# Two hybrid decoder layers on one core: the scheduler orders all engines but TensorE by a timeline simulation

## The chip, the cores and the metric

The kernel runs on one core of one Trainium2 chip. The metric is device microseconds of one execution; the runs give 2353.19, 2354.23 and 2355.81 us, median 2354.23. A core has a matrix engine (TensorE, PE in the profile; PEld is its weight load), three engines for elementwise work (VectorE or DVE, ScalarE or ACT, GpSimd or POOL) and SyncE (SP), which here issues all DMAs. Each engine takes its instructions in the order in which they stand in its own program, and waits on semaphores for the others.

## The reference, cut to what matters

```python
# x (1, 1024, 1024) f32, two layers; 4 mLSTM heads and 4 retention heads of 256; chunks
for l in range(DEPTH):
    ada = c_act @ w_ada[l] + b_ada[l]
    shift, scale, gate = jnp.split(ada, 3, axis=-1)
    h = rmsnorm(x, norm_g[l]) * (1.0 + scale[:, None, :]) + shift[:, None, :]
    p = h @ w_in[l]
    mq, mk, mv, mo, mz, mi, mf, rq, rk, rv, rz = split_cols(p)
    qk = jax.nn.silu(causal_dwconv(jnp.concatenate([mq, mk], axis=-1), conv_w[l], conv_b[l]))
    cell = mlstm_chunkwise(...)            # scores, running state C, n, stabiliser m, per chunk
    y_m = jax.nn.sigmoid(mo) * head_layernorm(cell, gn_m[l], N_HEADS_MLSTM) * jax.nn.silu(mz)
    ret = retention_chunkwise(rotary(rq), rotary(rk), rv)   # scores with decay, running state R
    y_r = head_layernorm(ret, gn_r[l], N_HEADS_RET) * jax.nn.silu(rz)
    y = jnp.concatenate([y_m, y_r], axis=-1) @ w_out[l]
    x = x + gate[:, None, :] * y
return rmsnorm(x, final_g)
```

## The kernel before, in words

All products are made in about full f32 precision out of three matmuls (`mm3`, L134 to L136): each operand is split into a high part, which ScalarE casts to fp32r (L590), and the rest, which GpSimd (or in places VectorE) gets by a subtraction (L591). `split_to` does both, so nearly all splits have these two lines: weights (`raw` to `wH`, `wL`), scores (`sH`, `sL`), the running state (`cH`, `cL`), q and k (`b`).

A layer first normalises and transposes its input (`norm_scale` L291, `norm_transpose` L296, `norm_evac` L302/L304) into `hT`. Then come eight head groups `hg`, 0 to 3 mLSTM, 4 to 7 retention. Each has the products for the gates (`gate_path`, with `z_evac` L518/L520 and `o_evac` L529/L530, stored to `gdr` at L523 and L531), for q and k (`qk_ml` or `qk_ret`) and for v. The weights are loaded by `load_w_raw` on SP (L317) into four `raw` buffers and split into six `wH` and six `wL` buffers.

k goes through DRAM to be transposed: `k_store` writes `kdr` (L622), `k_rows` loads it back with four DMAs per chunk (L632) and splits it on ScalarE and VectorE (L641/L642 for mLSTM, L646/L648 for retention). `attention` takes four chunks of 256 rows: `scores(j)` (L742 in part, masked at L744 to L747), `values(j)` (evacuated at L788/L797/L799, statistics from L808, the variance at L818 to L825, normalised on ScalarE at L830), `update(j)` for the state (L766/L769), `finish(j)` to DRAM (`ndr`, L842). At the end of a layer `OutLoads` fetches the normalised rows and gates (L879, L880), multiplies and splits them (L882 to L886), and `out_units` makes the output product, which `out_evac` adds to x (L927 to L931). The last rows go out by `final_rows` (L960, L961, L966).

Generators carry this work: the products of one head group run as units (`run_units`), and after each unit `tick()` lets launched generators (attention of the previous group, k rows, the rotary tables during `hg` 1 of layer 0, the next layer's adaLN columns from `hg` 2 of layer 0 on, the output gate's rows from `hg` 5 on) write some of their own steps. So the text of the program interleaves the groups.

That written order is what TensorE executes: one line asks for it, and a second one does so for every engine during the startup:

```python
manual = ctx.enter_context(tc.manual_schedule(engines={mybir.EngineType.PE}))
startup = tc.manual_schedule()
startup.__enter__()
```

The startup holds the loads of x and of the first adaLN weights, and a `script` of some hundred short steps up to the first v weights of layer 0 (`startup.__exit__` follows it). After it, VectorE, ScalarE, GpSimd and SP are ordered by the framework's scheduler. It replays the program on a simulated machine; when an engine of that machine is free, it gets, of the instructions whose inputs and buffers are ready there, the one that stands earliest in the text. The order found so is written into each engine's program and does not change on the chip. The buffers of a pool (62 of the tag `b`, four `raw`, and so on) are given out along this replay, and so are the waits for buffers in use. One more constraint holds the four loads of the rotary tables (`load_rotary`) behind a store of head group 3 on SP. The simulated machine is the framework's default one, which carries its own estimate of each instruction's duration.

## Time and profile before

| what | value |
|---|---|
| runs | 2353.19, 2354.23, 2355.81 us |
| span of the profiled execution | 2353.8 us (the page gives no other time for it) |
| TensorE | 2307.7 us busy, 12597 matmuls |
| VectorE | 1289.8 us busy, 2699 instructions |
| ScalarE | 893.3 us busy, 1736 instructions |
| GpSimd | 882.8 us busy, 841 instructions |
| DMA | 260.50 MB, 111 GB/s on average |
| mean granted clock of TensorE | 0.994 |

A row of the waits names the waiting engine, tile and line, then who released it: the total in us, how often, the longest. A row of the timeline has its start and length in us, the engine, line and operation, the tile written and those read, and in brackets how long the engine stood idle before it and for whom. In a row of windows stand the stretch, its length, and the busy time of each engine with its number of instructions, then the granted TensorE clock, the share of the DMA engines in use, and GB/s. Numbers of buffers are left out of the names, so `b` stands for any of 62.

### The profile page before, as it was taken

What the parts mean: (1) busy time and instruction counts of PE and PEld (TensorE: products, weight loads), DVE (VectorE), ACT (ScalarE), POOL (GpSimd) and SP (SyncE); (2) the same over time, 40 slices, a digit from 0 to 9 for tenths busy, and PEclk for the clock granted to TensorE, in tenths of its full rate; (3) what the DMA queues carried; (4) which work ended last, traced back from release to release, by engine and by line L of the source; (5) the groups of instructions that cost most, each with busy time, mean ns of one, the idle gap of its engine ahead of it and who ended that gap; (6) DMA issues with size and microseconds to landing.
All of it is one profiled execution on the core that took longest, in us unless ns stands there. A gap on an engine that the chain in (4) does not pass through costs nothing.

```text
span 2353.8 us, 34446 instructions
## 1 busy us (share of the span) xinstructions
PE 2307.7 (98%) x12597; PEld 1982.2 (84%) x12597; DVE 1289.8 (55%) x2699; ACT 893.3 (38%) x1736; POOL 882.8 (38%) x841
## 2 busy tenths in 40 slices
PE   5999999999999999999999999999999999999998
PEld 4888888988978988988888888888898888888886
DVE  7375687656454445475525655454543444555753
ACT  5535443444332322343434444344443322224442
POOL 0344333443244343323453444343334434341313
PEclk8999999999999999999999999999999999999999
DMA  7223232434332433277422333322323242425762
GB/s 243 74 68 99 73 88 72 116 94 126 108 99 71 117 83 102 81 241 254 167 78 77 82 76 78 80 68 76 81 70 86 77 112 77 117 82 159 266 231 77
DMA packets 326971, 260.50 MB, mean 111 GB/s; under 512 B 75893, under 2 KB 262013, under 8 KB 326801
## 3 DMA queue, kind: packets, MB, share of 16 engines
q1 hardware_dynamic: 326800, 258.30, 37.4%
q8 instruction: 99, 1.62, 0.3%
q14 instruction: 72, 0.58, 0.1%
HBM read 202.61 MB, written 55.61 MB: 110 GB/s over the span
## 4 chain that ended last, share of the span: by engine, by line
PE 93%; DVE 2%; DMA 2%; issue 1%; POOL 1%; ACT 1%; SPq 1%; POOLq 0%; ACTq 0%; DVEq 0%
PE pp L134 24%; PE pp L136 24%; PE pp L135 24%; PE pa L136 6%; PE pa L134 6%; PE pa L135 6%; PE pa L742 1%; DMA b<-in_w_ada_dram 1%; DMA b<-in_x_dram 1%; PE pa L296 0%; DVE b L233 0%; DMA dm<-mdr 0%; POOL wL L591 0%; SPq L995 0%; POOL b L591 0%
## 5 line engine op out<-in xcount | busy, mean ns | idle before, releaser
L134 PE MATMUL pp<-b,wH 128*128 128x512 f32 x1792 | 712.7, 398 | 1.1 <-ACT b L1073 1.1
L135 PE MATMUL pp<-b,wH 128*128 128x512 f32 x1792 | 708.2, 395 | 1.3 <-DVE b L1076 1.3
L136 PE MATMUL pp<-b,wL 128*128 128x512 f32 x1792 | 708.2, 395 | 0.0
L591 POOL TENSOR_TENSOR wL<-raw,wH 128x512 fp32r<-128x512 f32 x338 | 449.2, 1336 | 578.5 <-ACT wH L590 506.5
L136 PEld LDWEIGHTS pp<-b,wL 128*128 128x128 f32 x1792 | 337.8, 189 | 81.0
L134 PEld LDWEIGHTS pp<-b,wH 128*128 128x128 f32 x1792 | 338.7, 189 | 74.1 <-issue 1.5
L135 PEld LDWEIGHTS pp<-b,wH 128*128 128x128 f32 x1792 | 338.4, 189 | 73.7 <-DVE b L1076 2.0
L590 ACT CAST wH<-raw 128x512 fp32r<-128x512 f32 x402 | 247.3, 617 | 390.4 <-PE pp L135 138.3
L136 PE MATMUL pp<-wH,b 128*128 128x256 f32 (+1 forms) x1152 | 353.0, 306 | 1.2 <-DVE b L886 1.1
L134 PE MATMUL pp<-wH,b 128*128 128x256 f32 (+1 forms) x1152 | 353.6, 307 | 0.0
L135 PE MATMUL pp<-wL,b 128*128 128x256 f32 (+1 forms) x1152 | 352.6, 306 | 0.0
L591 POOL TENSOR_TENSOR b<-acc,b 128x256 fp32r<-128x256 f32 (+1 forms) x208 | 200.4, 983 | 319.9 <-ACT b L590 306.0
L136 PEld LDWEIGHTS pp<-wH,b 128*128 128x128 f32 x1152 | 217.2, 189 | 13.5 <-DVE b L886 2.0
L134 PEld LDWEIGHTS pp<-wH,b 128*128 128x128 f32 x1152 | 216.9, 188 | 10.7
L135 PEld LDWEIGHTS pp<-wL,b 128*128 128x128 f32 x1152 | 216.6, 188 | 10.6
L590 ACT CAST b<-acc 128x256 fp32r<-128x256 f32 (+1 forms) x208 | 93.6, 487 | 201.5 <-DVE acc L685 136.5
L608 DVE SCALAR_TENSOR_TENSOR acc<-pp,cols,acc 128x511 f32<-128x511 f32 (+2 forms) x192 | 142.7, 743 | 44.2 <-ACT acc L603 42.0
L591 POOL TENSOR_TENSOR sL<-th,sH 128x384 fp32r<-128x384 f32 x64 | 69.5, 1086 | 155.4 <-ACT sH L590 141.2
L134 PE MATMUL pa<-wH,b 128*128 128x512 f32 x256 | 101.1, 395 | 0.0
L135 PE MATMUL pa<-wL,b 128*128 128x512 f32 x256 | 100.9, 394 | 0.0
L136 PE MATMUL pa<-wH,b 128*128 128x512 f32 x256 | 100.7, 393 | 0.0
L612 ACT ACTIVATE th<-acc 128x512 f32<-128x512 f32 x64 | 40.4, 632 | 146.6 <-DVE acc L610 79.8
(237 smaller groups left out, 3470.9 us busy)
## 6 DMA issues: line engine op xcount, KB each, us to landing
raw<-in_w_in_dram SPq DMA_DIRECT2D x274, 256.0 KB
raw<-in_w_out_dram SPq DMA_DIRECT2D x128, 256.0 KB
b<-in_w_ada_dram SPq DMA_DIRECT2D x96, 256.0 KB
gdr<-g SPq DMA_DIRECT2D x64, 256.0 KB
ndr<-zt SPq DMA_DIRECT2D x128, 128.0 KB
g<-ndr SPq DMA_DIRECT2D x64, 256.0 KB
g<-gdr SPq DMA_DIRECT2D x64, 256.0 KB
acc<-kdr SPq DMA_DIRECT2D x192, 64.0 KB
```

The costliest lines, as they stand in the source:

```text
L134: PE.matmul(o, lt[0], rt[0], start=start, stop=False)
L135: PE.matmul(o, lt[0], rt[1], start=False, stop=False)
L136: PE.matmul(o, lt[1], rt[0], start=False, stop=stop)
L590: A.copy(dst[0], src)
L591: eng.tensor_tensor(dst[1], src, f(dst[0]), ALU.subtract)
L608: V.scalar_tensor_tensor(acc[:, d:], pt[:, 0:HALF - d], wcol, acc[:, d:], ALU.mult, ALU.add)
L612: A.activation(th, acc, AF.Tanh, scale=0.5)
L742: PE.matmul(pd, kk[i][:, jo + P:jo + CH], qd, start=dt == 0 and i == 0, stop=dt == 1 and i == 1)
```

## The change

The context that traces and schedules the kernel is made with another setting: the machine on which the scheduler replays the program is the framework's timeline simulation instead of its default estimate. The program's text, its instructions, its tiles and pools, TensorE's order and the hand-ordered startup are the same.

```diff
-    with tile.TileContext(nc) as tc:
+    with tile.TileContext(nc, schedule_with_timeline_sim=True) as tc:
         tile_hybrid_trunk(tc, *args)
```

## The prediction

> **What bounds the kernel now.** I read the page's sections 1 and 4 first, then the windows table by stage, then TensorE's own waits stage by stage, then single rows around the longest of them.
>
> ```profile
> span 2353.8 us, 34446 instructions
> PE 2307.7 (98%) x12597; PEld 1982.2 (84%) x12597; DVE 1289.8 (55%) x2699; ACT 893.3 (38%) x1736; POOL 882.8 (38%) x841
> PE 93%; DVE 2%; DMA 2%; issue 1%; POOL 1%; ACT 1%; SPq 1%; POOLq 0%; ACTq 0%; DVEq 0%
> ```
>
> TensorE is busy for 98% of the span and holds 93% of the chain that ended last. The other engines have room: VectorE 55%, ScalarE and GpSimd 38% each. TensorE's own order is not touched by the change, so the question is only how long TensorE stands still. The windows give that by stage (core; us, busy PE, PEld, DVE, ACT, POOL; then granted clock, DMA share, GB/s):
>
> ```profile
> 0.00:60.00 60.00, 34.26 (x135) 26.88 (x136) 42.01 (x90) 30.44 (x58) 4.00 (x10) 0.87 0.74 239
> 60.00:120.00 60.00, 59.33 (x350) 52.05 (x349) 24.28 (x56) 33.57 (x64) 21.07 (x25) 0.96 0.28 73
> 120.00:1200.00 1080.00, 1071.51 (x5864) 920.71 (x5863) 621.79 (x1305) 396.47 (x771) 422.52 (x389) 1.00 0.39 114
> 1200.00:1260.00 60.00, 59.32 (x365) 52.28 (x364) 20.31 (x47) 23.31 (x57) 28.44 (x33) 1.00 0.28 83
> 1260.00:2340.00 1080.00, 1079.23 (x5874) 927.45 (x5874) 574.66 (x1188) 405.19 (x780) 404.85 (x381) 1.00 0.36 103
> 2340.00:2353.80 13.80, 4.02 (x18) 2.88 (x16) 6.76 (x17) 4.29 (x10) 1.95 (x3) 0.81 0.40 152
> ```
>
> The idle time of TensorE is 2353.8 - 2307.7 = 46.1 us. Row by row it is 25.74 + 0.67 + 8.49 + 0.68 + 0.77 + 9.78. The first two rows (26.4 us) are the startup, which the kernel orders by hand for all engines and which the change therefore leaves alone. The last row is the final evacuation behind the last matmul, a chain of dependent steps (add, square sum, root, scale, store) that another order hardly shortens. What the scheduler's order can touch is the middle: 8.49 + 0.68 + 0.77 = **9.94 us, or 0.42%**.
>
> The two long windows are the key. Layer 0 (120 to 1200) and layer 1 (1260 to 2340) run nearly the same program, 5864 and 5874 matmuls, and the scheduler ordered each for itself. One order leaves 8.49 us idle, the other 0.77.
>
> **The change part by part.** It adds and removes no instruction. Every one of the 2699 VectorE, 1736 ScalarE and 841 GpSimd instructions, and every DMA issue on SP, may change its place in its own queue, outside the startup. Buffers are handed out while the order is made, so which buffer a tile takes, and whom it waits for, may change too. I cost the edit by what the waits of TensorE can become. These are layer 0's (waiter, releaser: us in total, times, longest):
>
> ```profile
> PE pa L134 <- ACT b L646: 2.7, 1, 2.7
> PE pa L135 <- POOL cL L591: 2.1, 2, 1.2
> PE pp L136 <- DVE b L886: 1.1, 1, 1.1
> PE pa L134 <- ACT nd L788: 1.0, 1, 1.0
> PE pa L134 <- DVE nd L797: 0.7, 1, 0.7
> PE pa L136 <- POOL sL L591: 0.6, 1, 0.6
> PE pa L134 <- DVE th L745: 0.2, 1, 0.2
> ```
>
> Layer 1 has one named wait in its window:
>
> ```profile
> PE pa L136 <- POOL sL L591: 0.6, 1, 0.6
> ```
>
> *Step 1, the longest wait.* At 686 us TensorE waits for the split of k rows (L646):
>
> ```profile
> 674.99 3.90 SPq L632 DMA_DIRECT2D acc<-kdr  x8
> 679.49 1.28 ACT L518 ACT_TABLE_LOAD   x1
> 683.54 0.62 ACT L590 CAST wH<-raw 128x512 fp32r<-128x512 f32 x1
> 684.70 1.30 POOL L591 TENSOR_TENSOR wL<-raw,wH 128x512 fp32r<-128x512 f32 x1
> 684.82 1.19 DVE L824 TENSOR_TENSOR va<-mv,kc 128x2 f32<-128x2 f32 x1
> 687.02 1.02 ACT L830 ACTIVATE n<-pa,nmu,rsd 128x256 f32<-128x256 f32 x2 [2.86 <-DVE nmu L827]
> 688.93 1.15 ACT L646 ACTIVATE b<-acc 128x512 fp32r<-128x512 f32 x2
> 689.61 0.58 PE L134 MATMUL pa<-b,b 128*128 128x256 f32 x1 [2.74 <-ACT b L646]
> 690.00:695.00 5.00, 5.00 (x22) 4.37 (x22) 1.90 (x5) 1.45 (x4) 1.07 (x1) 0.70 0.72 194
> ```
>
> The eight loads of `acc<-kdr` were issued by 678.9. ScalarE was free from 684.2 on, but next in its order stood L830, which waited 2.86 us for VectorE, so L646 began only at 688.93. This is a place where order alone cost time: 2.74 us of standing still, and then a granted clock of 0.70 over 5 us, another 5 x 0.30 = 1.5 us; 4.2 us together. If the new order puts L646 ahead of L830, 4.2 us go, and the next thing due is the next matmul's weights, already there. If it does not, nothing moves.
>
> [...]
>
> *Step 2, the weight splits on GpSimd.* A state split `cL` (L591) gates the next chunk's matmuls, and GpSimd's commonest other work is the weight split:
>
> ```profile
> L591 POOL TENSOR_TENSOR wL<-raw,wH 128x512 fp32r<-128x512 f32 x338 | 449.2, 1336 | 578.5 <-ACT wH L590 506.5
> 1733.32 1.30 POOL L591 TENSOR_TENSOR wL<-raw,wH 128x512 fp32r<-128x512 f32 x1 [2.98 <-ACT wH L590]
> 1734.57 1.31 POOL L591 TENSOR_TENSOR cL<-cf,cH 128x516 fp32r<-128x516 f32 x1
> 1737.08 0.29 PE L135 MATMUL pa<-cL,b 128*128 128x258 f32 x1
> 1604.94 1.30 POOL L591 TENSOR_TENSOR cL<-cf,cH 128x516 fp32r<-128x516 f32 x1
> 1610.21 0.28 PE L135 MATMUL pa<-cL,b 128*128 128x258 f32 x1
> ```
>
> In layer 1 one state split ends at 1735.88 and is needed at 1737.08, a slack of 1.20 us; another ends at 1606.24 and is needed at 1610.21, 3.97 us. One weight split put ahead costs 1.34 us: 0.14 at the first place, nothing at the second. Two cost 1.47 and nothing. So the bounds of a wrong place here are 0 and about 1.5 us. Layer 0's two waits on `cL`, 2.1 us in two, are nearest; I take 1.05 for each new one.
>
> *Step 3, table loads and weight prefetch.* If the four Sin activations of the rotary tables were mixed with Tanh, ScalarE would pay 1.28 us for each further table load; weight casts and splits run ahead of TensorE in six buffers. Both lie beside matmuls in engines 38% busy, and I cost them at nothing. Were that cover gone, each load would cost its 1.28 us.
>
> *Sum.* Layer 0 carries the extra rotary and next-layer adaLN work whatever the order, and its waits can fall or rise; I keep its 8.49 us. Layer 1 is close to the floor and can only rise; I give it two waits of step 2's size, 2 x 1.05 = 2.1 us. The profiled execution's 2353.8 becomes 2355.9. The median of the runs, 2354.23, lies 0.4 above that span, so the forecast is **2356.3 us**. Its bounds come from the two layers: if both become like layer 1, 8.49 - 0.77 = 7.7 us go, and 1.5 of clock with them, 9.2 in all; if both become like layer 0, 9.2 are added. That is 2345 to 2363.
>
> **The rivals.**
>
> *Faster: the better simulation repairs layer 0.* For it: the wait of 2.74 us at 686 was a matter of order, and layer 1 shows that such an order exists. Against it: to pass 0.2% (4.7 us, about what a measurement of this kernel can tell from no change) the 4.2 us of step 1 do not suffice; a further wait must go and no new one come. It gives 2354.2 - 9.2 = 2345.0.
>
> *Slower: a weight load in front of the k rows on SP.* SP takes its DMAs strictly in its written order, and a weight load (L317) waits at its head for a free buffer:
>
> ```profile
> SPq L317 <- POOL wL L591: 811.2, 216, 24.7
> SPq L317 <- POOL wL L591: 29.9, 11, 9.2
> 1011.72 4.21 DMA g<-gdr
> ```
>
> The first row is the whole span, the second the stretch 600 to 700, the third one transfer of the chain. The k rows at step 1 had 689.61 - 678.9 = 10.7 us from their last issue to their use; less 4.2 for a landing (taken from the third row) and 1.2 for L646, 5.3 us are slack. A load put in front decides once it waits longer than 5.3 us. The mean, 811.2/216 = 3.8 us, is below that, which speaks against it; the 9.2 and the 24.7 speak for it. One wait of 9.2 costs 3.9 and the clock's 1.5, 5.4; two such places give 2365; one wait of 24.7 costs 19.4 + 1.5 = 20.9 and gives 2375. Behind the loads stand the stores of gates and normalised rows too, but nobody needs these before the output product.
>
> *Slower: VectorE caught behind GpSimd.* The two-column step L824 took 1.19 us at 684.82, in step with the weight split that ran from 684.70 to 686.00:
>
> ```profile
> L824 DVE TENSOR_TENSOR va<-mv,kc x32: 147/161/1191, 684.8 to 2198.5; 128x2 f32<-128x2 f32 x32
> ```
>
> Its median is 161 ns. So a weight split at the wrong moment adds 1.03 us to a chunk's chain. If the new order does so once in each of the 16 head groups and no slack is left there, 16 x 1.03 = 16.5 us and 2371. Against it: one in 32 does it now, and the slacks of step 2 are mostly larger. [...]
>
> *No effect at all.* Both simulations may pick orders that differ nowhere TensorE looks: 2354.2.
>
> **How the numbers follow.** Chances: forecast (a few waits exchanged, within 0.2%) 0.43; no effect 0.06; faster 0.17; SP rival 0.28; VectorE rival 0.06. That makes faster 0.17, same 0.49, slower 0.34. Both signs hold half of the chance, so the forecast's own range, 2350 to 2359, stands beside the full one: 2345 (both layers like layer 1) to 2375 (one longest load wait). About 2 in 10 lie outside, most of it above.
>
> **What would show it.** Right: TensorE busy within a few us of 2307.7, startup and tail rows unchanged, idle of the two long windows between 1.5 and 17 us together, waits of about 1 us each on `cL`, `sL`, `nd`. Step 1 shows in whether L646 starts ahead of L830 in the first retention head group. Step 2 is wrong if waits on `cL` exceed 1.5 us each. The SP rival would show as a wait of TensorE or ScalarE on `acc<-kdr` with an L317 wait ahead of it, and as windows of granted clock under 1. The prediction fails if TensorE's gaps number dozens, or if one lasts over 10 us.

## The result, and the profile after

The changed kernel ran in 2351.38 us (median of 15 runs, 2348.57 to 2353.24), the kernel before beside it in 2355.77 (15 runs, 2353.19 to 2358.19): a ratio of 0.9983, 95% interval 0.9975 to 0.9990. In a later series the same program gave 2347.5 against 2354.09, ratio 0.9971 (0.9962 to 0.9981). So it is faster, by 0.2 to 0.3%, where 0.1% slower was forecast; the range of 2345 to 2375 holds it. The narrower range of 2350 to 2359 holds the first series and not the later one; what the forecast missed in both is the direction. The profiled execution took 2348.77 us around a span of 2347.0.

TensorE's order is the same in both kernels, matmul for matmul. The page after, its first two lines:

```profile
span 2347.0 us, 34474 instructions
PE 2301.1 (98%) x12597; PEld 1980.3 (84%) x12597; DVE 1291.3 (55%) x2699; ACT 894.3 (38%) x1736; POOL 879.1 (37%) x841
```

Idle time of TensorE is 2347.0 - 2301.1 = 45.9 us, against 46.1 before: as a sum it has hardly moved. The windows after, in the columns of before (the last is cut at 2333, since this run ends 6.8 us earlier):

```profile
0.00:60.00 60.00, 33.00 (x140) 25.37 (x141) 42.64 (x90) 31.24 (x60) 3.99 (x10) 0.94 0.75 239
120.00:1200.00 1080.00, 1073.26 (x5876) 924.00 (x5875) 618.75 (x1310) 396.87 (x771) 419.86 (x389) 1.00 0.40 114
1260.00:2333.00 1073.00, 1071.85 (x5850) 923.38 (x5849) 579.12 (x1184) 400.91 (x774) 404.88 (x381) 1.00 0.37 104
```

Layer 0 stands idle for 6.74 us (8.49 before), layer 1 for 1.15 in a slightly shorter stretch (0.77). TensorE's waits, layer 0 and then layer 1:

```profile
PE pa L134 <- ACT nd L788: 4.1, 2, 2.2
PE pa L134 <- ACT n L830: 1.1, 1, 1.1
PE pa L135 <- POOL cL L591: 0.7, 1, 0.7
PE pa L484 <- DVE b L474: 0.7, 1, 0.7
PE pa L484 <- DVE b L474: 1.1, 1, 1.1
```

The wait for L646 (2.7 us) is gone, as are those for L886, L797 and `sL`. The wait for L788 has grown from 1.0 to 4.1, and one for L474 is new. So this is an exchange of waits with a small surplus. Busy time hides part of it, since a matmul at half clock counts as busy for longer: at L135, 128x256, a mean of 416 ns in the kernel before from 689.60 to 693.01 us, where the granted clock was 0.50, and 281 ns in the 3.4 us behind that at 1.00. The cleaner account is by matmul: since TensorE's order is the same, the time from the start of matmul i to the start of matmul k can be compared between traces. Worked out from the matmul records, us:

| matmuls (time before) | before | after | after, profiled again | what lies there |
|---|---|---|---|---|
| 0 to 149 (from 3) | 62.16 | 60.16 | 59.78 | startup, same hand-made order |
| 1570 to 1640 (326) | 15.71 | 13.38 | 13.38 | L788 behind masks, L797 behind rotary steps |
| 1640 to 1760 (342) | 23.85 | 26.00 | 29.05 | L788 behind the masks L728 |
| 2290 to 2340 (460) | 8.91 | 10.85 | 12.19 | L788 behind masks again, a head group later |
| 3570 to 3625 (683) | 14.45 | 11.21 | 10.44 | L646, step 1 of the prediction |
| 5450 to 5520 (1008) | 13.79 | 12.40 | 12.41 | L886, output product of layer 0 |
| 6860 to 6890 (1295) | 5.96 | 7.30 | 7.19 | L474, gate chain of layer 1 |
| 7080 to 7300 (1343) | 40.85 | 39.92 | 39.92 | `sL` in layer 1 |
| 7300 to 12300 (1384) | 890.88 | 889.38 | 889.38 | rest of layer 1 |
| tail | 10.14 | 9.85 | 9.85 | |

Won: 2.33 + 3.24 + 1.39 + 0.93 + 1.50 + 0.29 = 9.7 us. Lost: 2.15 + 1.94 + 1.34 = 5.4. Net 4.3, and stretches not listed add 0.4. The startup adds 2.0 that the change can't have made: three profiles with before's order (this one and two below) gave 58.2 to 62.2 us there, six with the new one 59.1 to 61.6. From matmul 149 to the end the new order stands at 2284.08 and 2286.65 us in its two profiles (the second is the slowest execution of its nine), the old one at 2288.74. Of these stretches those at 342, 460 and 683 us are put to the test by edits below; the others are read from the traces alone.

What the new order does can be seen in who waits for a DMA (whole span; first before, then after):

```profile
POOL dm L725 <- DMA dm<-mdr: 33.1, 19, 7.9
ACT dm L728 <- POOL dm L725: 33.4, 22, 3.2
ACT b L646 <- DMA acc<-kdr: 22.6, 12, 3.8
```

```profile
POOL dm L725 <- DMA dm<-mdr: 73.7, 26, 10.0
ACT dm L728 <- POOL dm L725: 60.1, 27, 4.8
ACT b L646 <- DMA acc<-kdr: 31.8, 22, 3.4
```

GpSimd waits 2.2 times as long for the mask loads, ScalarE 1.8 times as long for GpSimd's masks. Work that hangs on a load stands earlier in its engine's order than it did, at its head before the data are there. That reads as if the timeline simulation let transfers land sooner than the default does; no run looked into the simulation itself. Where the data are there in time it is a gain, as for L646; where not, the engine holds up whatever is ready behind, as for L788.

### The profile page after: what moved, and what is told of

Read it like the earlier page. It is cut to its first block, busy times and chain, and to the rows that moved or that the text cites. A ratio compares the mean times of both kernels' runs of the same rounds, so it can differ in the third digit from the quotient of the medians.

```text
span 2347.0 us, 34474 instructions
## 1 busy us (share of the span) xinstructions
PE 2301.1 (98%) x12597; PEld 1980.3 (84%) x12597; DVE 1291.3 (55%) x2699; ACT 894.3 (38%) x1736; POOL 879.1 (37%) x841
## 4 chain that ended last, share of the span: by engine, by line
PE 89%; DVE 5%; DMA 2%; issue 1%; ACT 1%; POOL 1%; SPq 0%; POOLq 0%; DVEq 0%; ACTq 0%
PE pp L134 23%; PE pp L136 23%; PE pp L135 23%; PE pa L134 6%; PE pa L135 6%; PE pa L136 6%; PE pa L742 1%; DMA b<-in_w_ada_dram 1%; DMA b<-in_x_dram 0%; PE pa L296 0%; POOL b L591 0%; DVE b L458 0%; DMA b<-in_w_in_dram 0%; DVE acc L608 0%; DMA rdr<-g 0%
## 5 line engine op out<-in xcount | busy, mean ns | idle before, releaser
L135 PE MATMUL pp<-b,wH 128*128 128x512 f32 x1792 | 707.8, 395 | 1.3 <-DVE b L1076 1.3
L135 PEld LDWEIGHTS pp<-b,wH 128*128 128x128 f32 x1792 | 338.3, 189 | 73.8 <-DVE b L1076 2.4
L135 PE MATMUL pp<-wL,b 128*128 128x256 f32 (+1 forms) x1152 | 353.1, 307 | 0.0
L135 PEld LDWEIGHTS pp<-wL,b 128*128 128x128 f32 x1152 | 217.2, 189 | 10.8
L135 PE MATMUL pa<-wL,b 128*128 128x512 f32 x256 | 101.0, 395 | 0.0
L591 POOL TENSOR_TENSOR cL<-cf,cH 128x516 fp32r<-128x516 f32 (+1 forms) x48 | 63.1, 1314 | 89.3 <-ACT cH L590 89.3
```

The source lines that it names most:

```text
L135: PE.matmul(o, lt[0], rt[1], start=False, stop=False)
L591: eng.tensor_tensor(dst[1], src, f(dst[0]), ALU.subtract)
```

## The experiments

All edits add edges of order between two instructions of one engine and nothing else; `order_after(a, b)` puts a behind b, and `marks` holds instructions by layer, head group, chunk. TensorE's order never changes. The two runs with k rows, the same order again and masks late share one series (before: 2354.09 us, 25 runs), the other three another (2355.01, 15 runs).

**The k rows early, in the kernel before.** The edges also put the neighbouring casts behind L646.

```diff
+ if (l, hg, j) == (0, 4, 0):
+     for m in (marks[0,4,1,'sH'], marks[0,4,0,'n',0], marks[0,4,0,'n',1]):
+         order_after(m, marks[0,4,0,'krow'])
+ # and two weight casts L590 and one tanh L518 likewise
```

> The kernel before with one place of ScalarE's order moved by hand: in layer 0, first retention head group (686 us), the split of the first k rows (L646) stands ahead of the normalisation L830 and of the cast of the next scores, as in the changed kernel; everything else keeps the default order. Theory A (the change's gain is this wait: 2.74 us of idle and 1.5 us of clock behind it, and the other exchanged waits cancel): TensorE's wait for L646 goes, the clock stays at 1.00 there, and the time falls by 4.2 us, to about 2351.5 where the kernel before has 2355.8. Theory B (the gain is spread over many small places, or lies in the startup's clock, where the two profiles differ by 2.1 us): under 1.5 us.

Measured: 2350.49 us, ratio 0.9985 (0.9976 to 0.9994). ScalarE's timeline (start, length, engine, line, operation, tile):

```profile
677.77 0.62 ACT L646 ACTIVATE b<-acc 128x512 fp32r<-128x512 f32 x1
680.03 0.63 ACT L646 ACTIVATE b<-acc 128x512 fp32r<-128x512 f32 x1
683.29 1.02 ACT L830 ACTIVATE n<-pa,nmu,rsd 128x256 f32<-128x256 f32 x2 [2.63 <-DVE nmu L827]
```

Both L646 are done before L830 begins to wait, TensorE has no wait left at this place, and the stretch from matmul 3570 to 3625 fell from 14.45 to 10.10 us: 4.35, against 4.2 by step 1. In this stretch one swap alone is worth about what the change nets behind the startup in its first profile, 4.66 us. Over the whole run it is worth less: other stretches gave back 1.2 us in this execution (2285.58 us from matmul 149 to the end, against 2288.74), and by the medians of this series the swap took 3.6 us where the change took 6.6.

**The k rows late, in the kernel after.**

```diff
+ if (l, hg, j) == (0, 4, 0): order_after(marks[0,4,0,'krow'], marks[0,4,0,'n',1])
```

> The changed kernel with the same place put back: L646 of the first chunk stands behind L830 again. Theory A: TensorE waits there 2 to 3 us more, with a clock under 1 behind it, and the time rises by 3 to 4.4 us over the changed kernel, back to within 1 us of the kernel before. Theory B: within 1 us of the changed kernel.

Measured: 2351.7 us, ratio 0.9993 (0.9984 to 1.0002); the unchanged order in the same series 2347.5. From ScalarE's and TensorE's timelines and the windows:

```profile
686.89 1.02 ACT L830 ACTIVATE n<-pa,nmu,rsd 128x256 f32<-128x256 f32 x2 [2.71 <-DVE nmu L827]
687.80 0.63 ACT L646 ACTIVATE b<-acc 128x512 fp32r<-128x512 f32 x1
688.49 0.39 PE L134 MATMUL pa<-b,b 128*128 128x256 f32 x1 [2.90 <-ACT b L646]
688.00:693.00 5.00, 4.49 (x24) 3.79 (x25) 3.57 (x8) 3.64 (x8) 2.64 (x2) 1.00 0.42 121
```

The wait is back with 2.90 us, and the stretch takes 13.29 us, 2.1 to 2.9 more than in the two profiles of the unchanged order. But the granted clock after the gap stayed at 1.00, where before's 2.74 us were followed by 0.70. So the wait belongs to the order, the clock's 1.5 us only sometimes. The medians differ by 4.2, as expected, but the time is not back to within 1 us of the kernel before (2354.09); the 1.3 to 2.1 us beyond this stretch weren't traced to a place. Three of the 11 runs lie at 2355.8 to 2356.8 us, the others at 2349.2 to 2353.5. The profiled one (2349.75) is among the shorter, so what the longest did at this place isn't seen.

**The same order again.**

> The changed kernel once more, on the same chip as the three above, as their base and for a second profile. Theory A: 0.17% under the kernel before, as measured; the first 100 us of its profile may differ from the first profile's by 2 us either way, and the waits of about 2 us at 345, 462 and none at 686 repeat to within 0.3 us. Theory B: the startup again ends some 2 us earlier than in the profile of the kernel before.

Measured: 2347.5 us (9 runs). The span of its profile is 2349.2, so 2.2 above the first profile of the same program. From TensorE's timeline and the windows:

```profile
346.18 0.58 PE L134 MATMUL pa<-b,b 128*128 128x258 f32 x1 [3.13 <-ACT nd L788]
346.00:351.00 5.00, 4.82 (x17) 4.21 (x18) 4.97 (x16) 1.49 (x4) 1.99 (x2) 0.50 0.48 123
```

At the mask place this execution waited 3.13 us and went on at a clock of 0.50; the first one, shown below, waited 2.17. The waits were expected to repeat to within 0.3 us; this one is off by 0.96. Two executions of one order differ there by 3.05 us (29.05 to 26.00). Elsewhere they mostly agree within 0.1; the exceptions are the second mask place (1.34), the L646 place (0.77), a stretch at 138 us (0.92) and the startup (0.38). The startup is again over 2 us shorter than in before's profile, as the rival expected; but the other two profiles of before's order have 58.2 and 59.9 us there, so the new order is not the reason.

**Masks early, in the kernel before.** This is the losing half of the change by itself.

```diff
+ if (l, hg, j, tt) == (0, 2, 1, 1):          # at the mask L728
+     for i in range(2): order_after(marks[0,1,2,'nd',i], marks[0,2,1,'mask',1])
```

> The kernel before, with one swap of the change alone: on ScalarE at 346 us both mask exponentials L728 of the coming head group stand ahead of both L788, as the timeline simulation has them (before: L788, L728, L788, L728). Theory (the early masks are what the change lost at this place): the first L788 starts not at 346.6 but behind the second mask, at about 351.5 us, TensorE needs it at 348.3: a wait of 3 to 4 us and up to 1.5 us at half clock, so the stretch 342 to 366 us rises from 23.8 by 3.0 to 5.3 us and the whole by as much, to 1.0013-1.0023 of before. Rival (the loss there came from other differences of the order and the masks are at the place by then): under 0.5 us.

First the two orders as they ran, ScalarE and the matmul that waits; before:

```profile
346.60 0.48 ACT L788 ACTIVATE nd<-pa,wd 128x258 f32<-128x258 f32 x1
349.84 0.51 ACT L728 ACTIVATE dm<-dm,COL 128x256 f32<-128x256 f32 x1 [2.76 <-POOL dm L725]
350.25 0.46 ACT L788 ACTIVATE nd<-pa,wd 128x258 f32<-128x258 f32 x1
348.26 0.28 PE L134 MATMUL pa<-b,b 128*128 128x258 f32 x1
```

and after, with the window behind the gap:

```profile
343.86 0.51 ACT L728 ACTIVATE dm<-dm,COL 128x256 f32<-128x256 f32 x1 [3.87 <-POOL dm L725]
344.67 0.40 ACT L728 ACTIVATE dm<-dm,COL 128x128 f32<-128x128 f32 x1 [0.31 <-POOL dm L726]
344.98 0.82 ACT L788 ACTIVATE nd<-pa,wd 128x258 f32<-128x258 f32 x2
345.49 0.39 PE L134 MATMUL pa<-b,b 128*128 128x258 f32 x1 [2.17 <-ACT nd L788]
345.00:350.00 5.00, 4.38 (x18) 3.81 (x19) 4.96 (x15) 1.81 (x5) 2.30 (x2) 0.66 0.43 113
```

The mask is that of the coming head group, written some thousand instructions later in the text. Before, the first L788 slips in ahead of it and TensorE does not wait; after, both masks stand in front. The experiment, same views:

```profile
348.06 0.51 ACT L728 ACTIVATE dm<-dm,COL 128x256 f32<-128x256 f32 x1 [3.39 <-POOL dm L725]
349.21 0.40 ACT L728 ACTIVATE dm<-dm,COL 128x128 f32<-128x128 f32 x1 [0.64 <-POOL dm L726]
349.52 0.82 ACT L788 ACTIVATE nd<-pa,wd 128x258 f32<-128x258 f32 x2
350.03 0.58 PE L134 MATMUL pa<-b,b 128*128 128x258 f32 x1 [3.64 <-ACT nd L788]
350.00:355.00 5.00, 4.97 (x18) 4.49 (x19) 4.56 (x19) 1.35 (x3) 1.99 (x2) 0.50 0.22 52
```

2359.28 us, ratio 1.0018 (1.0009 to 1.0027). The swap brings a wait of 3.64 us and half clock; the stretch from 1640 to 1760 goes from 23.85 to 28.93, 5.1 us, at the upper end of what was expected. The early masks are shown as a cause of a loss here.

**Masks late, in the kernel after.**

```diff
+ if (l, hg, j) in ((0, 1, 2), (0, 2, 1)):
+     for tt in range(2): order_after(marks[l,hg,j+1,'mask',tt], marks[l,hg,j,'nd',1])
```

> The changed kernel with two places of ScalarE's order moved by hand, at 345 us (head group 1) and 462 us (head group 2) of layer 0: the exponentials of a later chunk's mask (L728), which wait for a mask loaded by DMA, stand behind the evacuations L788 of the present chunk. Theory A (single heads of ScalarE's queue, each worth its own idle time and the clock behind it): TensorE's waits for L788 (4.1 us in two) go, and the half-speed stretch behind the first, about 1.7 us more; the time falls by 4 to 6 us under the changed kernel, to 2345.5 to 2347.5. Theory B: under 1.5 us.

Measured: 2345.8 us (5 runs, 2341.15 to 2348.57), ratio 0.9962 (0.9949 to 0.9974), 1.7 under the unchanged order and not the gain of 4 to 6 us expected. The first edge holds the mask of (0, 1, 3), and the one that blocked is that of (0, 2, 1); it follows the other through the two `dm` buffers. The place at 460 us is repaired, 8.66 us. What the change had altered there was not ScalarE's order, though: before, both masks stand ahead of L788 too (461.05, 461.91, then 462.73) and TensorE doesn't wait. Counted from matmul 149, TensorE comes there 0.4 us sooner after the change (397.81 for 398.23) and L788 1.5 us later (399.18 for 397.70), as does VectorE's L747 (393.58 for 392.12), for which the load of the mask waits. The place at 345 is not repaired:

```profile
342.27 0.43 DVE L378 TENSOR_TENSOR g<-g,g 128x256 f32<-128x256 f32 x1 [1.29 <-DMA rdr<-g]
345.12 0.43 DVE L797 TENSOR_TENSOR nd<-pa,nd 128x258 f32<-128x258 f32 x1
345.60 0.58 PE L134 MATMUL pa<-b,b 128*128 128x258 f32 x1 [3.52 <-DVE nd L797]
```

L788 was done by 339.1, but on VectorE a rotary step that waits for a store (L378) and four more rotary steps stand ahead of L797. A second engine held the same chain at the same place; the wait only changed its name.

**Masks and rotary step late, in the kernel after.** The edges of the run before, and:

```diff
+ if (n, which) == (1, 0): order_after(rot, marks[0,1,2,'add',1])   # rot: L378, 'add': L797
```

> The order found with the timeline simulation, with the two mask edges of the run before (masks L728 of the next chunk behind L788, twice in layer 0) and one more: on VectorE the rotary step L378, which waits for a store of the previous table to leave its buffer, now stands behind the two L797 of the same chunk. Theory (an engine in order holds what is ready behind what waits for a DMA, and at 342 to 346 us two such heads of queue lie side by side, the mask on ScalarE and the rotary step on VectorE): with both moved, TensorE's wait of 3.5 us for L797 at 345 us goes with its half-clock stretch, the stretch 342 to 366 us falls from 26.8 to 23.3-23.8 us, and the whole to 2341-2343 us. Rival (the attention chain is late anyway, so that the wait only moves to its next step): the stretch falls by less than 1 us and the whole stays at 2345-2346 us.

Measured: 2340.23 us (2339.10 to 2341.72), ratio 0.9936 (0.9924 to 0.9949): it beats both kernels. Timelines, and the windows of the two layers:

```profile
340.19 0.48 ACT L788 ACTIVATE nd<-pa,wd 128x258 f32<-128x258 f32 x1 [0.40 <-PE pa L136]
343.59 0.42 DVE L797 TENSOR_TENSOR nd<-pa,nd 128x258 f32<-128x258 f32 x1
120.00:1200.00 1080.00, 1078.72 (x5911) 928.87 (x5911) 624.53 (x1323) 399.42 (x778) 423.38 (x390) 1.00 0.40 115
1260.00:2325.00 1065.00, 1064.88 (x5820) 917.33 (x5819) 571.59 (x1179) 395.92 (x766) 406.31 (x380) 1.00 0.37 105
```

L788 and L797 now follow the matmuls; the stretch takes 21.76 us, below the 23.3 to 23.8 expected, because the old order had waits there too (1.3 us). Layer 0 keeps 1.28 us of idle time. At least 0.64% was to be had from order in this kernel; the change alone reached 0.2 to 0.3.

**Rotary step late alone, in the kernel after.**

> The order found with the timeline simulation, with the VectorE edge alone (rotary step L378 behind the two L797), the masks on ScalarE left where the simulation put them. Theory (two heads of queue side by side): TensorE is still released by L788 behind the masks, at the same place of the program, so the stretch 342 to 366 us stays at 26.0-29.1 us, within 0.5 us of what the unchanged order gives for the same wait of L788, and the whole stays at 2347-2351 us. Rival (VectorE alone holds the chain): the stretch falls by 2 to 3 us, as with both edges.

Measured: 2345.03 us, ratio 0.9960 (0.9948 to 0.9973), below what the theory allowed. TensorE, VectorE and the window:

```profile
345.15 0.38 PE L134 MATMUL pa<-b,b 128*128 128x258 f32 x1 [1.71 <-ACT nd L788]
345.13 0.43 DVE L797 TENSOR_TENSOR nd<-pa,nd 128x258 f32<-128x258 f32 x1 [3.76 <-ACT nd L788]
345.00:350.00 5.00, 4.85 (x27) 4.21 (x28) 4.48 (x16) 1.47 (x4) 1.82 (x2) 1.00 0.33 80
```

As expected TensorE is still released by L788 behind the masks, and VectorE now stands idle for it. But the stretch fell from 26.00 to 23.76 us, by 2.2, which is the size that the rival (VectorE alone holds the chain) had given. The rows don't bear the rival out: the wait for L788 is 0.46 us shorter, within the 1 us by which waits here vary in one order, and the clock stays at 1.00 where it was 0.66, about 1.7 us of 5. In the last section the step with this wait has 1.71 us of idle time, 0.03 less than the shortest that was followed by half clock in these traces, so this part hangs on a few hundredths of a microsecond. What stands is that only the run with both edges has 21.76.

## Why the prediction was wrong, point by point

**The bound** was right for the idle time and too narrow for the gain. TensorE is 98% busy, and startup and tail are not the scheduler's (the tail moved by 0.29 us). But 9.94 us, 0.42%, was called all that order could touch, and masks and rotary late took 0.64% with order alone. From matmul 149 to the last one it needs 13.4 us less than the kernel before (2265.19 for 2278.60): 7.6 us of that were idle time (10.61 to 2.96), the other 5.8 had been counted as busy, and the range allowed 1.5 of clock for that. With both edges, 1.28 + 0.12 us of idle time are left in the two windows.

**Step 1** was right in place and near in size. L646 now starts ahead of L830, and the swap alone gave 4.35 us against 4.2. Its two terms aren't equally firm: the wait of 2.74 belongs to the order, the 1.5 of clock did not come when the order was put back. The text left open whether the new order would make the swap; it did, and the sum did not count it.

**The step that failed is the sum**: "I keep its 8.49 us" for layer 0, and for layer 1 "can only rise", two waits of 1.05. Layer 0 was not kept but exchanged, 2.33, 3.24 and 1.39 us won against 2.15 and 1.94 lost. Layer 1 did not rise by 2.1. From the L474 wait on it changed by +1.34 - 0.93 - 1.50 - 0.29 = -1.4 us. Of the 1.50, two short waits make 0.66 (`sL` at 2049 us, the output product at 2160); the other 0.84 is spread over 5000 matmuls, under 0.2 ns each. The idle time did not fall below 0.77, as the prediction had it; what fell was time counted as busy, which its sum did not look at. Nor was 0.77 a floor: with both edges layer 1, ordered there as in the changed kernel, has 0.12. That the forecast was only 5 us off is luck: gains of 9.7 us and losses of 5.4 that it did not have partly cancelled.

**Step 2** named `cL` as the place where new waits would come: 2.1 us of it before, 0.7 after. The new waits came on the chain of L788, behind masks that wait for a load, at L830 and at L474; no term of the sum had these. **Step 3** holds: no wait of TensorE comes from a table load or a weight cast.

**From span to median** 0.4 us was added. The executions here lie 1.8 us above their span (2348.77 and 2347.0), so before's profiled execution took about 2355.6, close to the 2355.77 of the larger series. Counted so, the forecast would have been 2357.7, and further off.

**The rivals.** A better order in layer 0 came true in part: the L646 wait went and a further one (L797), which is what its condition asked for, but new ones came. SP's weight load decided none of the waits traced here. The nearest thing to it, from the timeline and from SP's waits between 600 and 700 us:

```profile
686.37 0.63 ACT L646 ACTIVATE b<-acc 128x512 fp32r<-128x512 f32 x1 [3.30 <-DMA acc<-kdr]
690.83 1.02 ACT L830 ACTIVATE n<-pa,nmu,rsd 128x256 f32<-128x256 f32 x2 [2.40 <-DVE nmu L827]
SPq L632 <- DMA kdr<-th: 3.7, 1, 3.7
```

ScalarE waits 3.30 us for a third chunk's k rows, but their load was held on SP by the store of the same rows, not by a weight load, and ScalarE then still waits 2.40 for VectorE before L830, for which TensorE waits its 1.1.

VectorE caught behind GpSimd shows in this very wait, on the chain to L830:

```profile
687.98 0.78 DVE L824 TENSOR_TENSOR va<-mv,kc 128x2 f32<-128x2 f32 x1
689.50 1.27 POOL L591 TENSOR_TENSOR wL<-raw,wH 128x512 fp32r<-128x512 f32 x1
689.56 1.23 DVE L827 SCALAR_TENSOR_TENSOR nmu<-mv,rsd 128x2 f32<-128x2 f32 x1 [0.81 <-POOL rsd L825]
```

L827 ran beside this split, L824 beside one of `sL` (687.48 to 688.74); each has a median of 161 ns, so the two lost 1.7 us on the way to L830, more than the 1.08 that TensorE waited. That is read from the rows and not tested. In the other profile of this order they were as slow and TensorE stood idle for 0.34 us. So this rival came true at one place and cost at most 1.1 us, not 1.03 in each of 16 head groups; L824 itself has a longest of 776 ns after, 1191 before. "No effect" is excluded by the orders and by the interval.

## What to carry to other kernels

When another cost model reorders the engines, look for instructions that wait at the head of an engine's order, for a DMA as at the masks or for another engine as at L830, and for what ready work stands behind them. In the kernel before, swaps at these two places changed their stretches by 5.1 and 4.35 us. Compare two orders of one program between the same matmuls, not by idle sums, since half clock counts as busy and waits change places. When a wait survives the removal of its named cause, look for a second engine that is blocked at the same point before giving the theory up; here ScalarE and VectorE each held the same chain, and only both edges together brought it to the matmuls' pace.

## What the runs showed of the hardware

The clock after a gap is not settled by the gap's length alone. Waits of 1.74, 2.17, 2.74, 3.13, 3.52 and 3.64 us were followed by 5 us windows at 0.66, 0.66, 0.70, 0.50, 0.66 and 0.50; waits of 1.71, 1.89, 2.24 and 2.90 were followed by 1.00. The records of the granted clock in the nine traces show where it changed. All its changes within a trace lie on a grid of 3.41 us: in the changed kernel's first profile, for instance, at 62.45, 345.76 and 349.17 us, 83 steps and one step apart; in the kernel before's at 64.96, 689.60 and 693.01, 183 steps and one. Where the grid lies differs from execution to execution. Cut along it, from matmul 149 to the last one, every step at full clock in which TensorE stood idle for 1.74 us or more was followed by one at half clock (eight of them, 1.74 to 3.01 us; among them 2.73 in the step at 686.19 us of the kernel before and 2.17 in the one at 342.34 of the changed kernel), and none with 1.71 us or less was. That is read off these traces; no edit was made to test it. The two steps nearest to each other, each with the step that follows, from the same order again and from rotary late alone:

```profile
461.25:464.67 3.42, 1.68 (x10) 1.10 (x9) 0.49 (x2) 2.35 (x6) 1.50 (x3) 1.00 0.24 86
464.67:468.08 3.41, 3.41 (x14) 3.12 (x14) 2.39 (x12) 0.81 (x2) 1.34 (x3) 0.50 0.32 77
342.49:345.90 3.41, 1.70 (x11) 1.17 (x10) 0.73 (x2) 2.08 (x6) 1.93 (x3) 1.00 0.17 54
345.90:349.31 3.41, 3.41 (x20) 2.91 (x20) 3.41 (x13) 0.57 (x2) 1.29 (x1) 1.00 0.38 92
```

The wait of 2.90 us was split by the grid into 1.57 and 1.34 us, and the clock stayed at 1.00. From the step's length and the clock of 0.50, a half-clock step costs an estimated 3.41 x 0.5 = 1.7 us, near the 1.5 of step 1.

The startup, the same instructions in the same order on every engine, took 58.2 to 62.2 us over nine profiles. That alone is 0.17% of the kernel, as much as the change in its first series. And the long stretch of layer 1 without waits (matmul 7300 to 12300) repeats to 0.01 us in five profiles of the new order, 889.38, while a sixth, k rows late, has 888.95 though its order there is the same by line and tile. The three profiles of before's order differ from one another there only by two short waits (890.88 to 891.48); without these two, before's stands 0.84 us above the new one, with the same matmuls. What does this stays open.
